# A fourth inner pair in seven products in every second gate and up group, and matrix products of the MLP tied to written order

## Chip, core and metric

The kernel runs on one core of one Trainium2 chip. The time is device time in microseconds (us), the median of several executions of the one program; before the change it is 1436.71 us (three runs, 1436.64 to 1439.13). Five engines work side by side, each through its own queue of instructions: TensorE (PE in the profile, its weight loads PEld), VectorE (DVE), ScalarE (ACT), GpSimd (POOL) and SyncE (SP, which here only issues transfers). Semaphores make one engine wait for another.

## The reference

One layer of an encoder over 256 rows of width 2048 in float32: four mixers side by side, cross attention, and the SwiGLU MLP that this change touches.

```python
D_MODEL = 2048
SEQ = 256
D_FF = ((8 * D_MODEL // 3 + 255) // 256) * 256      # 5632
...
def swiglu(h, w_gate_up, w_down):
    gate, up = jnp.split(h @ w_gate_up, 2, axis=-1)
    return (jax.nn.silu(gate) * up) @ w_down

def reference(x, mem, norm_g, w_in, ...):
    ...
        x = x + mix @ w_out[l]
        x = x + cross_attention(rms_norm(x, norm_g[l, 1]), mem_n, w_xq[l], w_xkv[l], w_xo[l])
        x = x + swiglu(rms_norm(x, norm_g[l, 2]), w_gate_up[l], w_down[l])
    return rms_norm(x, final_norm_g)
```

## The kernel before

**A product in three matmuls.** Float32 precision comes from splitting. Each operand is a high part (rounded to the type fp32r by a cast) and a low part (what the cast left). A product is high by high, high by low and low by high: the three matmuls of `part`, lines 433 to 435, each 128x128 by 128x512. Line 434 is the one that reads the low part `wl` of the weights.

**The weights as a stream.** The host lays all weights out in the order in which they are used, in slabs of 128x2048 (16 blocks of 128 columns). `Stream._load` fetches a slab into `raw` (three buffers); `Stream._half` casts 1024 columns of it to `wh` on ACT (line 135) and forms `wl` = `raw` − `wh` on DVE (line 136). Such a piece of `wh` and `wl` is called a half here. Four halves have buffers at a time: three of `wp` and one of `extra`. So the cast of a half can start only when TensorE is through with the half four places before it.

**Plain and paired slabs.** A group of the gate and up product takes 512 columns of gate and 512 of up, over 16 inner blocks of 128 (k), for 2 halves of the rows. A slab holds four blocks (k, column). Its plan has one letter per slab. "N", plain: 4 blocks by 2 row halves is 8 products, 24 matmuls, in two halves of the weights. "S", paired: two k by two column halves by two row halves by Winograd's variant of Strassen's scheme, 7 products in place of 8, 21 matmuls. Sums of weight blocks take the place of four of the blocks and sums of activations (`combine`, into the tiles `z`) the place of the activations. A paired slab makes four halves, or phases, 0 to 3: 1024, 512, 1024 and 1024 columns, used by 6, 3, 6 and 6 matmuls (`Stream._sums`, cast in line 159, low part in line 160). Before phase 2, DVE adds up weights in place in `raw` (line 157): four additions of 128x512, each reading what an earlier one wrote. Where the slab is in `SUMMED`, two transfers (`two`, line 101) and one accumulating transfer that POOL issues (line 102) do half of it, and DVE has two additions left.

**The groups.** Group 0 of gate and up is all plain (`gemm_rows`); while it runs, `combined` makes the sums of activations in the background. Groups 1 to 10 run the plan `GROUP` = "NNSNSNSN": five plain slabs and three paired ones, all three in `SUMMED`. After its last paired slab and at its end a group has a row of work on DVE: `mixed` puts the products together (four operations of 128x512), `gated` adds to the gate, `upped` adds to the up part, `up` multiplies (line 287) and `store_turned` transposes (line 557): twelve operations of 128x512. The result goes to memory in transposed order and is fetched back and split by the background task `fetch` (f and act tiles, 128x256) as operands of the down product.

**Down.** Two passes over 1024 columns each (`PASSES`), with the four-addition form of "S". The activation sums are made as they are needed; the last of the seven right operands (`x4` in `paired_rows`) is written into the slot of the first of the two inner blocks. `down_end` ends the kernel: four matmuls with the identity (line 1244) add what `mixed` left in `split` to the second half of the rows, then twelve inner blocks run for the first half of the rows, then for the second, each followed by `norm`.

**What sets the order.** The framework (Tile) places the instructions in each engine's queue when the program is built, by its own estimate of when each is ready; on the chip each queue runs in that order. `keep_place` adds edges without semaphores that tie an instruction behind the one written before it on the same engine. Before the change `down_end` has them around its four identity matmuls, and nothing ties the products of `paired_rows`.

Of the kernel before, what the change touches and what calls it, by code (L numbers as in the profile page):

```python
# [14 lines left out]
F32R = mybir.dt.float32r  # L15
# [8 lines left out]
P = 128  # L24
# [3 lines left out]
DFF = 5632  # L28
# [13 lines left out]
LATE = 12  # L42

GATE_UP = 1920 // 16 + 8
GROUP = "NNSNSNSN"

DOWN = GATE_UP + 80
PASSES = "NNNNSNNSNNSNNSNNSNNSNN", "NSNSNSNSNSNSNSNSNSNNNN"

PAIRED = {a + i for a, plan in [(GATE_UP + 8 * j, GROUP) for j in range(10)] + [(DOWN, PASSES[0]), (DOWN + 22, PASSES[1])]  # L50
          for i, x in enumerate(plan) if x == "S"}
SUMMED = {i for i in PAIRED if i < DOWN}

LAG, OWED, SOON, FAR = 1.3, 0.9, 0.01, 18.0
V_NG = 0
# [16 lines left out]
class Stream:  # L72
# [39 lines left out]
    def _half(self):  # L112

        nc, n = self.nc, self.made
        if n % 16 == 0 and self.phase == 0:
            self._load(n)
        if n // 16 in PAIRED:
            return self._sums()
# [74 lines left out]
    def take_sums(self, w, ks, cols):  # L193

        assert self.n // 16 in PAIRED and self.n % 16 == 0
        self.order += [(w, ks[k], cols[c] + i * P) for k, c in ((1, 0), (0, 0), (1, 1), (0, 1)) for i in range(4)]
# [58 lines left out]
class Block:  # L255
# [208 lines left out]
    def paired_rows(self, w, cols, slots, sums, plan, mixed, first, ready=None, late=0, before=None, swap=False):  # L464

        st, s, nk = self.st, len(sums), len(slots)  # L470
        rest = [k for k in range(nk) if not any(k in ks for ks, _ in sums)]
        steps = [(c, k) for c in range(2) for k in rest]
        todo, q = iter(sums), {}
        count = {"a0": len(rest) + s, "a1": len(rest) + s, "b0": len(rest) + s, "b1": len(rest)}
        left, total = {}, 0

        def put(name, hi, lo, wh, wl):
            if name not in q:
                for x in [name] if name in count else "1675":
                    q[x] = (self.bank if (name in count) == swap else self.gbank)()  # L480
                    left[x] = count.get(x, s)
            new = left[name] == count.get(name, s)
            left[name] -= 1
            self.part(q[name][:, :], hi, lo, wh, wl, new, left[name] == 0)

        form = lambda t, r: (t[:, r * P:(r + 1) * P], t[:, R + r * P:R + (r + 1) * P])
        n = done = 0
        for i, kind in enumerate(plan):
            if before:
                before(i)  # L490
            if kind == "S":
                ks, z = next(todo)
                a = [form(slots[ks[0]], 0), form(slots[ks[1]], 0), form(slots[ks[1]], 1)]
                hi, lo, x4 = self.forms(z, slots[ks[0]])
                x1, s2, s3 = ((hi[:, i * P:i * P + P], lo[:, i * P:i * P + P]) for i in range(3))
                t = (("5", x1), ("7", s3))
                pairs = iter((("1", a[0]), ("b0", x4), ("a0", a[1]), *(t if st.n // 16 in SUMMED else t[::-1]), ("a1", a[2]), ("6", s2)))
                for parts in st.take_sums(w, ks, cols):
                    for wh, wl in parts:
                        name, (hi, lo) = next(pairs)  # L500
                        put(name, hi, lo, wh, wl)
                        self.bg.poll()
                done += 1
                if done == s:
                    mixed(*(q[i] for i in "1567"))
            else:
                for c, k in steps[n:n + 4]:
                    if ready:
                        ready(k)
                    wh, wl = st.take(w, k, cols[c], 4)  # L510
                    for r in range(2):
                        put("ab"[c] + str(r), *form(slots[k], r), wh, wl)
                        self.bg.poll()
                n += 4
            if first and done == s and n >= len(rest):
                first(q["a0"], q["a1"])
                first = None
        assert n == len(steps) - late and done == s
        return [q["b0"], q["b1"]], rest[len(rest) - late:]
# [527 lines left out]
    def gate_up(self, gp, f, z):  # L1047

        nc = self.nc
        box, g, stored = {}, {}, []  # L1050

        def gate(ps):
            for r in range(2):
                g[r] = gp.tile([P, 512], F32, name=f"g{r}", tag=f"g{r}")
                nc.scalar.activation(g[r], ps[r], AF.Silu, scale=box["col"][:, r:r + 1])

        def up(j, ps, h=None):
            h = h or [gp.tile([P, 512], F32, name="h", tag="h", bufs=2) for _ in range(2)]
            for r in range(2):
                self.stt(h[r], ps[r], box["col"][:, r:r + 1], g[r], ALU.mult, ALU.mult)  # L1060
                self.store_turned(self.ff, 4 * j, r, g[r], h[r])
            stored.append(self.bg.now)

        def mixed(q1, q5, q6, q7):

            g[0], g[1], h[0], h[1] = (gp.tile([P, 512], F32, name=n, tag=n, bufs=b) for n, b in (("g0", 1), ("g1", 1), ("h", 2), ("h", 2)))
            nc.scalar.copy(g[0], q1)
            self.tt(h[0], g[0], q6, ALU.add)
            self.tt(g[1], h[0], q7, ALU.add)
            self.tt(h[0], q5, h[0], ALU.subtract)  # L1070
            self.tt(h[1], q5, g[1], ALU.subtract)

        def gated(*ps):

            for r in range(2):
                self.tt(g[r], g[r], ps[r], ALU.add)
                nc.scalar.activation(g[r], g[r], AF.Silu, scale=box["col"][:, r:r + 1])

        def upped(j, ps):

            for r in range(2):
                self.tt(h[r], h[r], ps[r], ALU.add)
            up(j, h, h)

        h = {}

        def fetch(k0, k1, ahead, pause, wait=0):

            m = {}
            for k in range(k0, k1 + ahead):  # L1090
                if k < k1:
                    while len(stored) <= k // 4:
                        yield
                    m[k] = self.tmp()
                    self.load_turned(m[k], self.ff, k)
                if k >= k0 + ahead:
                    while wait and self.bg.now < stored[(k - ahead) // 4] + wait:
                        yield
                    mark = self.mark()
                    self.split(f[k - ahead], m.pop(k - ahead))  # L1100
                    self.keep_place(mark)
                    self.have = k - ahead + 1
                    yield pause

        def norm():

            mark = self.mark()
            nc.scalar.activation(self.mg[:, 0:1], self.mg[:, 0:1], AF.Silu)
            self.keep_place(mark)
            yield 2.0  # L1110
            self.row_norm(1, box)
            yield

        arrival = lambda: gp.tile([P, R], F32, name="ar", tag="ar", bufs=4)
        last = self.bg.add(self.arrive(self.xf[1], 3, arrival, self.put3, FAR), go=True)
        col = self.bg.add(norm())

        def combined():
            for ks, z in sums:
                yield 3.0  # L1120
                yield from self.combine(z, *(self.h3[k] for k in ks))

        sums = [((2 * i, 2 * i + 1), z[i]) for i in range(GROUP.count("S"))]
        comb = self.bg.add(combined())
        ps = self.gemm_rows("w_gate_up", [0, DFF], self.h3,
                            parts=[(range(8), [0]), (range(8, 12), [0]), (range(12), [1]), (range(12, 16), [0]), (range(12, 16), [1])],
                            before=lambda n: n in (1, 3) and self.bg.drain(self.late if n == 1 else last))
        self.bg.drain(col)
        gate(ps[0])
        up(0, ps[1])  # L1130
        early = self.bg.add(fetch(0, FT - 22, 3, 2.0, 15))
        self.bg.drain(comb)
        for j in range(1, DFF // 512):
            upped(j, self.paired_rows("w_gate_up", [j * 512, DFF + j * 512], self.h3, sums, GROUP, mixed, gated, swap=j % 2 == 0)[0])
        self.bg.drain(early)
        self.fetch = self.bg.add(fetch(FT - 22, FT, 6, SOON))

# [73 lines left out]
    def down_end(self, f, ss, ps, rest, split):  # L1211
# [29 lines left out]
        mark = self.mark()  # L1241
# [7 lines left out]
        for r in range(2):  # L1249
# [4 lines left out]
            for c in range(3):  # L1254
                x = self.half(c, r)
                self.stt(x, x, 0.375, fg[:, c * 512:(c + 1) * 512], ALU.mult, ALU.mult)
        nc.scalar.mul(fg[:, 3 * 512:4 * 512], fg[:, 3 * 512:4 * 512], 0.375)
        for r in range(2):
            for k, wh, wl in held:
                self.part_rows(ps[r], r, f[k], wh, wl, False, k == FT - 1)  # L1260
            norm(ps[r], r)


# [627 lines left out]
```

## Time and profile before

| | |
|---|---|
| median of 3 runs | 1436.71 us |
| the profiled execution's own time | 1435.07 us |
| its span in the trace | 1433.3 us |
| TensorE, busy share of the span, instructions | 99%, 6589 |
| VectorE | 80%, 1738 |
| ScalarE | 57%, 1183 |
| GpSimd | 16%, 306 |
| granted TensorE clock | 0.999 |
| groups 1 to 10 of gate and up | about 778 to 1193 us of the span |
| down | about 1193 to 1424 us |

In the profile, a row of the timeline gives the start in us, the duration in us, engine, line, operation, output<-inputs (buffer numbers left out), shapes and count, and in brackets the idle time before it with what ended it. Durations overlap where an engine is pipelined: a matmul of 128x512 has a duration of 0.39 us, and the next starts 0.227 us after it. The time that an operation costs is therefore read from start to start. A row of the windows view gives the busy time of PE, PEld, DVE, ACT and POOL in that stretch with the count of instructions, then the granted clock, the busy share of the DMA engines and GB/s.

### The profile page before, as it was taken

How to read it: one execution, taken by the hardware profiler on the slowest of the kernel's cores; microseconds unless marked ns; L12 is line 12 of the kernel's file. 1: busy time of each engine (PE TensorE's matmuls, PEld its weight loads, DVE VectorE, ACT ScalarE, POOL GpSimd, SP SyncE). 2: the span in 40 equal slices, each digit the busy share in tenths (PEclk: the TensorE clock that was granted, in tenths of full speed). 3: DMA queues.
4: the chain of work that ended last, by engine and by line, in shares of the span. 5: the costliest groups of instructions: out<-in, count | busy, mean ns of one | idle time of the engine just before them, and what ended most of it. 6: DMA issues, size and time to landing. Idle time of an engine off the chain costs nothing.

```text
span 1433.3 us, 18652 instructions
## 1 busy us (share of the span) xinstructions
PE 1423.0 (99%) x6589; PEld 1180.7 (82%) x6589; DVE 1146.2 (80%) x1738; ACT 815.2 (57%) x1183; POOL 234.8 (16%) x306
## 2 busy tenths in 40 slices
PE   9999999999999999999999999999999999999997
PEld 8888888888888888888888888888888888888886
DVE  6667868777877767777677888898888888989997
ACT  7556565446645555556554656555555556655655
POOL 0000100013212223531431121122011002000000
PEclk9999999999999999999999999999999999999999
DMA  9876564546667788964986999889999887655554
GB/s 352 299 285 248 205 206 162 175 169 224 202 196 236 234 267 252 274 200 166 289 239 209 286 286 277 278 275 282 294 293 288 268 260 229 219 230 179 193 218 147
DMA packets 73037, 343.79 MB, mean 240 GB/s; under 512 B 10957, under 2 KB 12654, under 8 KB 45168
## 3 DMA queue, kind: packets, MB, share of 16 engines
q1 hardware_dynamic: 54848, 288.98, 57.5%
q0 software_dynamic: 17664, 52.97, 15.8%
q8 instruction: 51, 0.84, 0.2%
q10 hardware_dynamic: 432, 0.66, 0.1%
q14 instruction: 42, 0.34, 0.1%
HBM read 322.12 MB, written 20.45 MB: 239 GB/s over the span
## 4 chain that ended last, share of the span: by engine, by line
PE 97%; DVE 1%; ACT 0%; DMA 0%; issue 0%; SPq 0%; ACTq 0%
PE pg L433 22%; PE pg L434 22%; PE pg L435 22%; PE pm L434 7%; PE pm L435 7%; PE pm L433 7%; PE pg L381 4%; PE pg L382 2%; PE pm L1344 1%; PE pm L1022 1%; PE pm L993 1%; DMA raw<-in_W 0%; PE pm L1753 0%; DVE res L283 0%; PE pm L994 0%
## 5 line engine op out<-in xcount | busy, mean ns | idle before, releaser
L136 DVE TENSOR_TENSOR wl<-raw,wh 128x1024 fp32r<-128x1024 f32 (+1 forms) x413 | 494.8, 1212 | 166.1 <-ACT wh L135 163.2
L135 ACT CAST wh<-raw 128x1024 fp32r<-128x1024 f32 (+1 forms) x413 | 424.5, 1043 | 283.9 <-PE pg L435 196.4
L433 PE MATMUL pg<-wh,act 128*128 128x512 f32 (+1 forms) x1191 | 465.6, 391 | 0.0
L434 PE MATMUL pg<-wl,act 128*128 128x512 f32 (+1 forms) x1191 | 463.9, 389 | 0.4 <-DVE wl L136 0.2
L435 PE MATMUL pg<-wh,act 128*128 128x512 f32 (+1 forms) x1191 | 463.9, 389 | 0.0
L433 PEld LDWEIGHTS pg<-wh,act 128*128 128x128 f32 x1191 | 223.8, 188 | 47.8 <-issue 1.5
L434 PEld LDWEIGHTS pg<-wl,act 128*128 128x128 f32 x1191 | 223.8, 188 | 47.2 <-DVE wl L136 1.3
L435 PEld LDWEIGHTS pg<-wh,act 128*128 128x128 f32 x1191 | 223.7, 188 | 47.2 <-DVE act L283 0.4
L159 ACT CAST wh<-raw 128x1024 fp32r<-128x1024 f32 (+1 forms) x150 | 137.0, 921 | 146.8 <-DVE raw L157 46.4
L160 DVE TENSOR_TENSOR wl<-raw,wh 128x1024 fp32r<-128x1024 f32 (+1 forms) x150 | 156.1, 1061 | 57.0 <-ACT wh L159 56.8
L434 PE MATMUL pm<-wl,act 128*128 128x512 f32 x309 | 120.5, 390 | 0.1
L433 PE MATMUL pm<-wh,act 128*128 128x512 f32 x309 | 120.2, 389 | 0.0
L435 PE MATMUL pm<-wh,act 128*128 128x512 f32 x309 | 120.2, 389 | 0.0
L381 PE MATMUL pg<-act,wh 128*128 128x512 f32 x256 | 90.5, 395 | 0.0
L382 PE MATMUL pg<-act,wl 128*128 128x256 f32 x256 | 71.8, 280 | 0.0
L434 PEld LDWEIGHTS pm<-wl,act 128*128 128x128 f32 x309 | 58.0, 188 | 13.0 <-DVE wl L136 0.6
L433 PEld LDWEIGHTS pm<-wh,act 128*128 128x128 f32 x309 | 58.0, 188 | 12.0
L435 PEld LDWEIGHTS pm<-wh,act 128*128 128x128 f32 x309 | 58.0, 188 | 12.0
L102 POOL DMA_DIRECT2D two<-in_W x30 | 26.6, 887 | 241.2 <-DMA two<-in_W 116.0
L157 DVE TENSOR_TENSOR raw<-raw 128x512 f32<-128x512 f32 x90 | 62.0, 689 | 1.3
L159 ACT CAST wh<-two 128x1024 fp32r<-128x1024 f32 x30 | 31.6, 1052 | 51.1 <-PE pg L435 21.7
L381 PEld LDWEIGHTS pg<-act,wh 128*128 128x128 f32 x256 | 48.1, 188 | 10.5
(375 smaller groups left out, 1821.9 us busy)
## 6 DMA issues: line engine op xcount, KB each, us to landing
raw<-in_W SPq DMA_DIRECT2D x216, 1024.0 KB, 5.6
raw<-in_W SPq DMA_DIRECT2D x30, 768.0 KB, 6.1
two<-in_W SPq DMA_DIRECT2D x60, 256.0 KB, 4.9
two<-in_W POOLq DMA_DIRECT2D x30, 512.0 KB, 9.3
raw<-in_W SPq DMA_DIRECT2D x11, 512.0 KB, 7.6
hidden<-g POOLq DMA_DIRECT2D x22, 256.0 KB, 3.7
tmp<-hidden POOLq DMA_DIRECT2D x44, 128.0 KB, 5.4
features<-tmp POOLq DMA_DIRECT2D x32, 128.0 KB, 5.3
```

Source lines behind the costliest of these rows:

```text
L102: nc.gpsimd.dma_start(t, W[:, 512:1536], accum_op=ALU.add)
L135: nc.scalar.copy(wh[:, a:b], r[:, a:b])
L136: nc.vector.tensor_tensor(out=wl[:, a:b], in0=r[:, a:b], in1=wh[:, a:b].bitcast(F32), op=ALU.subtract)
L157: nc.vector.tensor_tensor(out=out, in0=a, in1=b, op=ALU.add)
L159: nc.scalar.copy(wh, src)
L160: nc.vector.tensor_tensor(out=wl, in0=src, in1=wh.bitcast(F32), op=ALU.subtract)
L381: self.nc.tensor.matmul(p[:, :], wh, slot[:, :], start=start, stop=False)
L382: self.nc.tensor.matmul(p[:, 0:R], wl, slot[:, 0:R], start=False, stop=stop)
L433: self.nc.tensor.matmul(p, hi, wh, start=start, stop=False)
L434: self.nc.tensor.matmul(p, hi, wl, start=False, stop=False)
L435: self.nc.tensor.matmul(p, lo, wh, start=False, stop=stop)
L993: nc.tensor.matmul(p[:, :], q[d][:, r * P:(r + 1) * P], kt[d][:, :], start=d == 0, stop=False)
```

## The change

Every second group gets a plan with four paired slabs: "NSNSsNSN", in groups 2, 4, 6, 8 and 10. The small "s" is a paired slab that isn't in `SUMMED`: its weights come in one plain transfer and DVE makes all four additions. A fourth tile `z3` takes the activation sums of the fourth pair, made in group 0. Each product in `paired_rows`, and the products of `down_end`, are tied to written order by `keep_place`.

```diff
-GROUP = "NNSNSNSN"
+GROUPS = "NNSNSNSN", "NSNSsNSN"
...
-PAIRED = {a + i for a, plan in [(GATE_UP + 8 * j, GROUP) for j in range(10)] + [(DOWN, PASSES[0]), (DOWN + 22, PASSES[1])]
-          for i, x in enumerate(plan) if x == "S"}
-SUMMED = {i for i in PAIRED if i < DOWN}
+PAIRED = {a + i for a, plan in [(GATE_UP + 8 * j, GROUPS[j % len(GROUPS)]) for j in range(10)] + [(DOWN, PASSES[0]), (DOWN + 22, PASSES[1])]
+          for i, x in enumerate(plan) if x in "Ss"}
+SUMMED = {GATE_UP + 8 * j + i for j in range(10) for i, x in enumerate(GROUPS[j % len(GROUPS)]) if x == "S"}
...
+            mark = self.mark()
             self.part(q[name][:, :], hi, lo, wh, wl, new, left[name] == 0)
+            self.keep_place(mark)
...
-            if kind == "S":
+            if kind in "Ss":
...
-        sums = [((2 * i, 2 * i + 1), z[i]) for i in range(GROUP.count("S"))]
+        z = z + [gp.tile([P, 1024], F32R, name="z3")]
+        sums = [((2 * i, 2 * i + 1), z[i]) for i in range(4)]
...
-            upped(j, self.paired_rows("w_gate_up", [j * 512, DFF + j * 512], self.h3, sums, GROUP, mixed, gated, swap=j % 2 == 0)[0])
+            plan = GROUPS[(j - 1) % len(GROUPS)]
+            upped(j, self.paired_rows("w_gate_up", [j * 512, DFF + j * 512], self.h3, sums[:8 - plan.count("N")], plan, mixed, gated,
+                                      swap=j % 2 == 0)[0])
...
         for r in range(2):
+            mark = self.mark()
             for k, wh, wl in held:
                 self.part_rows(ps[r], r, f[k], wh, wl, False, k == FT - 1)
+            self.keep_place(mark)
             norm(ps[r], r)
```

## The prediction

> **What bounds the kernel now.** I read the page's busy times, then its chain, then the windows over the MLP.
>
> ```profile
> span 1433.3 us, 18652 instructions
> PE 1423.0 (99%) x6589; PEld 1180.7 (82%) x6589; DVE 1146.2 (80%) x1738; ACT 815.2 (57%) x1183; POOL 234.8 (16%) x306
> PE 97%; DVE 1%; ACT 0%; DMA 0%; issue 0%; SPq 0%; ACTq 0%
> ```
>
> TensorE is busy from end to end and holds 97% of the chain. A matmul that goes saves its time, and a matmul that waits adds its wait; nothing else counts. What matters is how far VectorE, which must have `wl` ready, is from becoming late.
>
> ```profile
> 750.00:775.00 25.00, 25.00 (x112) 20.68 (x112) 17.93 (x27) 14.40 (x20) 0.00 (x0) 1.00 0.58 200
> ...
> 975.00:1000.00 25.00, 25.00 (x112) 20.71 (x111) 22.84 (x29) 14.83 (x18) 5.86 (x7) 1.00 0.86 260
> ```
>
> In the all-plain group 0 DVE works 17.9 of 25 us; in the mixed groups 22.8. The mean leaves 2 us, but four halves of buffer are all the slack there is, so the order inside a group decides. That it is short of slack already shows in the chain, in group 4:
>
> ```profile
> 914.50 1.06 ACT wh L159
> 915.58 1.24 DVE wl L160
> 916.86 0.50 PE pm L434
> ```
>
> That is phase 3 of the first paired slab: PE waited there for the low part, and the slab had two plain slabs before it.
>
> **Removed matmuls.** Each fourth pair turns 24 matmuls into 21. Five groups: 15 fewer. Window 975 to 1000 holds 112 matmuls in 25 us, 0.223 each; the rows below (985.58 to 993.51, 35 steps) give 0.2266. So **−3.4 us**. The transferred bytes are the same, and the new activation sums run in group 0, under the idle 7 us in 25 of its DVE: nothing.
>
> **First paired slab of a changed group.** Group 6 begins at 985.58 in the trace and is one of the changed. I lay the built program's new DVE queue on its old times.
>
> ```profile
> 985.58 0.39 PE L433 MATMUL pm<-wh,act 128*128 128x512 f32 x1
> ...
> 993.51 0.39 PE L435 MATMUL pm<-wh,act 128*128 128x512 f32 x1
> ```
>
> ```profile
> 993.98 1.05 ACT L159 CAST wh<-two 128x1024 fp32r<-128x1024 f32 x1 [1.78 <-issue]
> ```
>
> ```profile
> 978.14 3.50 DVE L136 TENSOR_TENSOR wl<-raw,wh 128x1024 fp32r<-128x1024 f32 x3 [0.21 <-ACT wh L135]
> ...
> 985.72 1.23 DVE L136 TENSOR_TENSOR wl<-raw,wh 128x1024 fp32r<-128x1024 f32 x1
> 986.87 0.68 DVE L283 TENSOR_TENSOR g<-g,pg 128x512 f32<-128x512 f32 x1
> ...
> 991.20 1.19 DVE L136 TENSOR_TENSOR wl<-raw,wh 128x1024 fp32r<-128x1024 f32 x1
> 992.31 1.82 DVE L160 TENSOR_TENSOR wl<-raw,wh 128x1024 fp32r<-128x1024 f32 x2
> 994.04 0.42 DVE L283 TENSOR_TENSOR f<-tmp,f 128x256 fp32r<-128x256 f32 x1
> 994.38 0.69 DVE L157 TENSOR_TENSOR raw<-two,raw 128x512 f32<-128x512 f32 x1
> 995.07 1.23 DVE L160 TENSOR_TENSOR wl<-two,wh 128x1024 fp32r<-128x1024 f32 x1
> 996.21 0.69 DVE L157 TENSOR_TENSOR raw<-raw 128x512 f32<-128x512 f32 x1
> ...
> 998.09 1.23 DVE L160 TENSOR_TENSOR wl<-raw,wh 128x1024 fp32r<-128x1024 f32 x1 [1.19 <-ACT wh L159]
> ```
>
> Reading them: a matmul started at 993.51 was the last on its half, and the cast into that buffer came at 993.98, so a buffer is free 0.24 us after the half's time (993.74) is over. DVE runs without a pause from 978.14 to 996.9: that is the previous group's tail, of which 4.33 us (986.87 to 991.20) stand in one piece. From start to start a half costs DVE 1.14 us (and is done 0.1 later), a short one 0.60, an addition 0.69, or 0.61 where nothing hangs on it. Phase 3 is ready at 999.3, and PE reads it at 985.58 + 48 + 15 + 1 matmuls = 1000.1: 0.8 us to spare.
>
> In the new plan one plain slab is gone from in front: PE wants phase 3 at 985.58 + 40 × 0.2266 = 994.65. The same tail ends at 991.20 (the slot at 985.72 now holds the slab's phase 0). Then phase 1 (0.60), addition (0.61), phase 2 (1.14), addition (0.69): 994.24. The cast (1.05) ends at 995.4, and the built queue puts both halves of the *next* plain slab in front of phase 3 in groups 2, 6 and 10 (slab and phase after each `wl`, "add" for line 157):
>
> ```
> ... transposes; wl 1S.1; add; wl 1S.2; add; wl 2N.a; wl 2N.b; wl 1S.3; wl 3S.0 ...
> ... wl 4s.0; wl 4s.1; add; add; add; add; wl 4s.2; wl 5N.b; wl 4s.3; wl 5N.a ...
> ```
>
> 994.24 + 3 × 1.14 + 0.1 = 997.75: **3.1 us** late. In groups 4 and 8 one half is in front: 995.5 + 1.14 + 0.1, 2.1 us late. (With none it would be 2.0: the tail alone does that.)
>
> **The "s" right behind an "S".** Its phase 0 takes the buffer of the S's phase 0 and all four additions wait for it.
>
> ```profile
> 1393.28 2.87 DVE L157 TENSOR_TENSOR raw<-raw 128x512 f32<-128x512 f32 x4
> 1396.06 1.22 DVE L160 TENSOR_TENSOR wl<-raw,wh 128x1024 fp32r<-128x1024 f32 x1
> ```
>
> Four additions cost 2.78. From the end of S's phase 0: release 0.24, cast 1.05, low part 1.14, short one 0.60, additions 2.78, phase 2 1.14, 0.1: 7.05 us. PE needs it after 3 + 6 + 6 + 6 + 3 + 1 matmuls, 5.67: **1.4 us** late. Then one half of the next slab and phase 3, 2.28 us, against six matmuls, 1.36: **0.9** more. Between the two places N gives DVE time to catch up, so they add: 5.4 us in three groups, 4.4 in two, **+25.0 us**. Bounds: if only one of the two places waits, 11 to 14; nothing hidden and weights late, up to 5 more, since a 1 MB transfer took
>
> ```profile
> raw<-in_W SPq DMA_DIRECT2D x4, 1024.0 KB, 7.5
> ```
>
> 7.5 us to land, and the "s" slab's is issued only when phase 3 of the first S is done, some 8 us before its cast. I take nothing for it.
>
> **Moved splits.** `fetch` now splits in the plain groups' last third; one 128x256 split (0.34 by the row at 994.04) falls into the tail before four of the five: **+1.3** (0 to 2).
>
> **Edges.** In gate and up the queue was in written order already; 0. In down the old queue ran other products while the operand `x4` was late:
>
> ```profile
> 1231.16 0.39 PE L433 MATMUL pg<-wh,act 128*128 128x512 f32 x1
> ...
> 1234.03 0.40 PE L435 MATMUL pg<-wh,act 128*128 128x512 f32 x1
> ```
>
> ```profile
> 1232.08 1.22 DVE L160 TENSOR_TENSOR wl<-raw,wh 128x1024 fp32r<-128x1024 f32 x1
> ...
> 1233.55 0.29 DVE L283 TENSOR_TENSOR act<-tmp,act 128x128 fp32r<-128x128 f32 x1
> ```
>
> Its last matmul stands at 1234.03, and by written order it is due at 1231.62. The new DVE queue does two operations of 0.34 before `x4` and one of 1.14 after it, so it comes at 1233.4: 1.8 late, less 0.3 lost there already, **+1.5** (0 to 2). DVE then has that time at the next pair, where 0.3 was lost: −0.3.
>
> At the end the old queue put 13 products of the first and second half of the rows before or between the identity matmuls, which wait for DVE:
>
> ```profile
> 1406.98 0.39 PE L433 MATMUL pm<-wh,act 128*128 128x512 f32 x1
> ...
> 1410.55 0.77 PE L1244 MATMUL pm<-tmp,identr 128*128 128x256 f32 x2
> 1411.15 0.39 PE L433 MATMUL pm<-wh,act 128*128 128x512 f32 x1
> ...
> 1424.30 0.39 PE L435 MATMUL pm<-held,act 128*128 128x512 f32 x1
> ```
>
> ```profile
> 1410.45 0.43 DVE L283 TENSOR_TENSOR tmp<-res,tmp 128x256 fp32r<-128x256 f32 x1
> ```
>
> The last identity matmul needs 1410.45 + 0.43. Tied, all 72 products start behind it: 1411.05 + 71 × 0.2266 = 1427.14 in place of 1424.30, **+2.8** (0 to 3.4; two DVE operations before it also change places).
>
> **Sum**: −3.4 + 25.0 + 1.3 + 1.2 + 2.8 = +26.9 on the profiled execution's 1435.07 (1.8 of it outside its span): 1462. The median of the runs shown is 1.6 above that execution: **1463.6**.
>
> **Rivals.**
> Faster: if DVE ran its queue far enough ahead at both places in a group, only −3.4 and the edges (+4.0 by the rows, 0 if the old reordering there bought nothing) would be left: 1433 to 1437. For it: DVE idles 2.2 us in 25, 3.6 in a group, plain groups could make up the rest, and an "s" slab needs only 4.5 more (3 × 1.14 + 0.60 + 2.78, against 2 × 1.14). Against: the slack is not where the work is; phase 3 had 0.8 us to spare and loses 5.4. It decides if phase 3 is ready by 994.65.
> Half: one place waits, the other is absorbed: 1436.7 − 3.4 + 13 + 5 = 1451.
> Weights late as well, 1 us at each of five "s" and as much behind them: 1463.6 + 10 = 1474. The 7.5 us above against 8 speak for it, that the landings in the groups before held up no matmul against it.
> Half clock: after a wait of 3 us the array could run slow. At the program's start it did:
>
> ```profile
> 5.72 0.40 PE L434 MATMUL pg<-wl,act 128*128 128x256 f32 x1
> 5.93 0.31 PE L435 MATMUL pg<-wh,act 128*128 128x256 f32 x1
> 6.08 0.28 PE L433 MATMUL pg<-wh,act 128*128 128x256 f32 x1
> 6.20 0.28 PE L434 MATMUL pg<-wl,act 128*128 128x256 f32 x1
> ```
>
> 0.21 a step, then 0.12, about 5 us into the work. Up to 5 us at half speed after each of five long waits costs 2.5 each: 1476. Against it: the waits are broken by matmuls. [...]
>
> **Chances.** Forecast, both places (1456 to 1471): 0.55. Half: 0.20. Late weights or half clock: 0.16. Faster rival: 0.09, of which 0.06 ends faster by over 0.2% (2.9 us, about what a measurement of this kernel tells from none) and 0.03 within it. Slower 0.91. The range, 1447 to 1475, leaves out the faster rival, the low end of Half and the top of the last: 0.19.
>
> **What would show it.** PE waiting for line 160 in phase 3 of the first S and in phases 2 and 3 of "s", five times each, about 5 us a group; plain groups still 41.5 us; the last matmul some 3 us later behind line 1244. It is wrong if changed groups last 40.8 us, or if waits stand mostly at DMA.

## The result, and the profile after

The changed kernel takes 1472.83 us (median of five runs, 1471.7 to 1475.43) against 1436.64 (five runs, 1435.42 to 1439.13): a ratio of 1.0252, 95% interval 1.0237 to 1.0267. It is 36.2 us slower, where 26.9 were forecast. The profiled execution took 1475.43 us.

From the page of the kernel after: the span, the busy times, the chain by engine, and the group of the low-part matmuls of the paired slabs.

```profile
span 1473.7 us, 18659 instructions
PE 1436.6 (97%) x6574; PEld 1181.1 (80%) x6574; DVE 1170.0 (79%) x1776; ACT 825.5 (56%) x1195; POOL 234.7 (16%) x306
PE 85%; DVE 8%; DMA 4%; issue 1%; ACT 1%; SPq 0%; ACTq 0%; DVEq 0%
L434 PE MATMUL pm<-wl,act 128*128 128x512 f32 x279 | 112.3, 402 | 11.7 <-DVE wl L160 11.7
```

There are 15 matmuls fewer and TensorE is busy 13.6 us longer, its share falls from 99% to 97%. VectorE's part of the chain goes from 1% to 8%, DMA's from 0% to 4%. The last row names the place: TensorE stood 11.7 us in front of matmuls that read `wl`, each time for line 160.

Windows of the kernel after, one row for each of groups 2, 3, 4, 6, 8 and 10:

```profile
820.13:866.69 46.56, 42.70 (x182) 33.47 (x180) 39.43 (x47) 23.08 (x27) 7.75 (x9) 1.00 0.87 256
866.69:908.17 41.48, 41.48 (x185) 34.35 (x183) 36.74 (x46) 25.74 (x32) 7.74 (x9) 1.00 0.93 286
908.17:955.98 47.81, 44.39 (x181) 34.42 (x180) 40.05 (x48) 24.61 (x28) 7.78 (x9) 0.96 0.84 250
997.46:1044.35 46.89, 42.70 (x182) 33.48 (x180) 40.12 (x48) 24.27 (x28) 5.99 (x7) 1.00 0.85 245
1085.83:1135.75 49.92, 45.67 (x182) 35.23 (x181) 41.71 (x51) 25.92 (x29) 5.88 (x7) 0.93 0.82 235
1177.23:1227.73 50.50, 44.53 (x181) 34.53 (x180) 40.90 (x50) 26.48 (x30) 4.28 (x5) 0.97 0.68 213
```

The plain group 3 lasts 41.48 us, as before, for 183 matmuls: 0.2267 each. A changed group has 180, nominally 40.81. What each has over that is 5.75, 7.01, 6.08, 9.11 and 9.70 us: 37.65 in five groups, of which 3.4 are given back by the matmuls saved. In groups 4, 8 and 10 the granted clock is under 1, of which more below. The last matmul starts at 1465.28, 40.98 after that of before (1424.30). The account: 0.96 ahead of group 1 (which starts between 777.7 and 779.4 in the profiles of this case, with and without the new plan); 33.7 in the groups; 1.4 in the first pass of down (118.03 us against 116.65); 4.95 in the second pass and the end.

The first paired slab of group 6, TensorE's timeline and then VectorE's (start and duration in us):

```profile
1004.94 0.39 PE L433 MATMUL pg<-wh,z 128*128 128x512 f32 x1
1005.81 0.50 PE L434 MATMUL pg<-wl,z 128*128 128x512 f32 x1 [0.48 <-DVE wl L160]
...
1006.84 0.39 PE L435 MATMUL pg<-wh,z 128*128 128x512 f32 x1
1007.50 0.50 PE L433 MATMUL pm<-wh,act 128*128 128x512 f32 x1 [0.27 <-ACT wh L159]
1009.82 0.50 PE L434 MATMUL pm<-wl,act 128*128 128x512 f32 x1 [1.82 <-DVE wl L160]
```

```profile
1003.37 0.65 DVE L160 TENSOR_TENSOR wl<-raw,wh 128x512 fp32r<-128x512 f32 x1
1003.94 0.68 DVE L157 TENSOR_TENSOR raw<-two,raw 128x512 f32<-128x512 f32 x1
...
1005.68 0.68 DVE L157 TENSOR_TENSOR raw<-raw 128x512 f32<-128x512 f32 x1
1006.28 2.35 DVE L136 TENSOR_TENSOR wl<-raw,wh 128x1024 fp32r<-128x1024 f32 x2
1008.55 2.35 DVE L160 TENSOR_TENSOR wl<-raw,wh 128x1024 fp32r<-128x1024 f32 x2
```

This is the queue that the prediction laid out: the two low parts of the next plain slab (line 136, at 1006.28) stand ahead of phase 3's at 1008.55, and TensorE, which began phase 3 at 1007.50, goes on at 1009.82. Phase 2 and the start of phase 3 had waited before (0.64 and 0.43 us by start to start). These waits belong to the same lateness: the slab is 3.44 us over nominal in all, and the prediction had phase 3 come 3.1 us late. By the same count the first pair is 3.09, 2.37, 3.44, 5.35 and 5.84 us over nominal in groups 2, 4, 6, 8 and 10. In groups 8 and 10 its weights came late. ScalarE in group 8 (from 1085.83), ScalarE in group 10 (from 1177.23), and VectorE behind the second:

```profile
1087.13 1.05 ACT L159 CAST wh<-raw 128x1024 fp32r<-128x1024 f32 x1 [3.64 <-DMA raw<-in_W]
```

```profile
1178.63 1.05 ACT L159 CAST wh<-raw 128x1024 fp32r<-128x1024 f32 x1 [4.62 <-DMA raw<-in_W]
```

```profile
1179.71 1.22 DVE L160 TENSOR_TENSOR wl<-raw,wh 128x1024 fp32r<-128x1024 f32 x1 [1.27 <-ACT wh L159]
```

The cast of the pair's phase 0 waits for the transfer, VectorE waits for the cast, and the rest of the previous group's row stands behind that low part in VectorE's queue. Phase 1's low part, which follows the row, came 5.6 to 5.9 us after the group's start in groups 2, 4 and 6 (5.91 in the rows above) and 7.9 and 8.0 us after it in groups 8 and 10. Behind an "S", the "s" of the same group:

```profile
1023.62 0.50 PE L433 MATMUL pg<-wh,z 128*128 128x512 f32 x1
1025.05 0.50 PE L434 MATMUL pg<-wl,z 128*128 128x512 f32 x1 [0.93 <-DVE wl L160]
...
1026.32 0.40 PE L433 MATMUL pm<-wh,act 128*128 128x512 f32 x1
1027.32 0.50 PE L434 MATMUL pm<-wl,act 128*128 128x512 f32 x1 [0.61 <-DVE wl L160]
```

0.25 before the first row, 1.20 and 0.78 after the two rows of line 433 (step less 0.2267): phase 2 and phase 3, about 2.5 us with the small rest in four of the five groups, against 2.3 forecast. Group 4 has 4.48: its wait before the first row's place is 1.14 in place of 0.25, and half clock (0.50, from 936.46) follows.

The end, TensorE's timeline:

```profile
1443.46 0.39 PE L435 MATMUL pm<-wh,act 128*128 128x512 f32 x1
1444.46 0.38 PE L1249 MATMUL pm<-tmp,identr 128*128 128x256 f32 x1 [0.61 <-ACT tmp L299]
1445.97 0.38 PE L1249 MATMUL pm<-tmp,identr 128*128 128x256 f32 x1 [1.13 <-DVE tmp L283]
1446.85 0.85 PE L1249 MATMUL pm<-tmp,identr 128*128 128x256 f32 x2 [0.49 <-ACT tmp L299]
...
1448.46 0.62 PE L434 MATMUL pm<-wl,act 128*128 128x512 f32 x1
1448.88 0.63 PE L435 MATMUL pm<-wh,act 128*128 128x512 f32 x1
```

The four identity matmuls (now line 1249) come one by one, each as its operand is ready: 0.78 + 1.40 + 0.76 + 0.35 = 3.3 us. Then eight matmuls run at 0.426 us a step, 1.6 us more.

### The profile page after: what moved, and what is told of

Read it like the earlier page. It is cut to its first block, busy times and chain, and to the rows that moved or that the text cites. A ratio compares the mean times of both kernels' runs of the same rounds, so it can differ in the third digit from the quotient of the medians.

```text
span 1473.7 us, 18659 instructions
## 1 busy us (share of the span) xinstructions
PE 1436.6 (97%) x6574; PEld 1181.1 (80%) x6574; DVE 1170.0 (79%) x1776; ACT 825.5 (56%) x1195; POOL 234.7 (16%) x306
## 4 chain that ended last, share of the span: by engine, by line
PE 85%; DVE 8%; DMA 4%; issue 1%; ACT 1%; SPq 0%; ACTq 0%; DVEq 0%
PE pg L433 20%; PE pg L435 20%; PE pg L434 20%; PE pm L434 5%; PE pm L435 5%; PE pm L433 5%; DMA raw<-in_W 4%; PE pg L381 4%; DVE wl L160 3%; PE pg L382 2%; DVE wl L136 2%; DVE raw L157 2%; PE pm L1351 1%; ACT wh L159 1%; PE pm L1024 1%
## 5 line engine op out<-in xcount | busy, mean ns | idle before, releaser
L136 DVE TENSOR_TENSOR wl<-raw,wh 128x1024 fp32r<-128x1024 f32 (+1 forms) x403 | 483.0, 1211 | 163.6 <-ACT wh L135 161.5
L135 ACT CAST wh<-raw 128x1024 fp32r<-128x1024 f32 (+1 forms) x403 | 414.9, 1042 | 280.2 <-PE pg L435 190.3
L159 ACT CAST wh<-raw 128x1024 fp32r<-128x1024 f32 (+1 forms) x170 | 156.0, 923 | 172.3 <-PE pg L435 66.1
L160 DVE TENSOR_TENSOR wl<-raw,wh 128x1024 fp32r<-128x1024 f32 (+1 forms) x170 | 177.7, 1061 | 53.9 <-ACT wh L159 53.7
L434 PE MATMUL pm<-wl,act 128*128 128x512 f32 x279 | 112.3, 402 | 11.7 <-DVE wl L160 11.7
L433 PE MATMUL pm<-wh,act 128*128 128x512 f32 x279 | 111.2, 399 | 1.4 <-ACT wh L159 1.4
L435 PE MATMUL pm<-wh,act 128*128 128x512 f32 x279 | 110.7, 397 | 0.0
L157 DVE TENSOR_TENSOR raw<-raw 128x512 f32<-128x512 f32 x110 | 75.6, 687 | 1.8
L434 PEld LDWEIGHTS pm<-wl,act 128*128 128x128 f32 x279 | 53.4, 191 | 27.5 <-DVE wl L160 16.5
L102 POOL DMA_DIRECT2D two<-in_W x30 | 26.9, 896 | 255.9 <-DMA two<-in_W 76.0
L433 PEld LDWEIGHTS pm<-wh,act 128*128 128x128 f32 x279 | 53.7, 193 | 15.1 <-ACT wh L159 3.6
L435 PEld LDWEIGHTS pm<-wh,act 128*128 128x128 f32 x279 | 53.7, 192 | 10.9
```

What stands on the lines that cost most here:

```text
L102: nc.gpsimd.dma_start(t, W[:, 512:1536], accum_op=ALU.add)
L135: nc.scalar.copy(wh[:, a:b], r[:, a:b])
L136: nc.vector.tensor_tensor(out=wl[:, a:b], in0=r[:, a:b], in1=wh[:, a:b].bitcast(F32), op=ALU.subtract)
L157: nc.vector.tensor_tensor(out=out, in0=a, in1=b, op=ALU.add)
L159: nc.scalar.copy(wh, src)
L160: nc.vector.tensor_tensor(out=wl, in0=src, in1=wh.bitcast(F32), op=ALU.subtract)
```

## Experiments

Theory at the start: the waits at the two places carry the loss, and the edges cost only in down and at the end. Rivals: the edges cause most of it; the fetch, moved by the new plan, makes weights late. All medians stand beside runs of the kernel before on the same chip (1436.2 to 1436.8).

| kernel | median, us | over before | ratio, 95% |
|---|---|---|---|
| both places of edges, old plan | 1444.96 | 8.6 | 1.0044 to 1.0080 |
| edges of the rows, old plan | 1438.51 | 2.1 | 1.0009 to 1.0027 |
| edges, identity matmuls later | 1439.86 | 3.5 | 1.0018 to 1.0037 |
| new plan, no edges | 1455.56 | 19.2 | 1.0120 to 1.0152 |
| only an early first pair, no edges | 1445.14 | 8.8 | 1.0033 to 1.0070 |
| only an "s" behind an "S", no edges | 1442.64 | 6.3 | 1.0028 to 1.0054 |
| new plan, no edges, stream order | 1457.15 | 20.8 | 1.0118 to 1.0155 |
| new plan, no edges, fetch spread | 1456.14 | 19.8 | 1.0103 to 1.0151 |
| new plan, edges of the rows | 1467.87 | 31.1 | 1.0201 to 1.0232 |
| after, fetch spread | 1466.67 | 29.9 | 1.0191 to 1.0228 |
| after, stream order | 1465.18 | 29.0 | 1.0175 to 1.0227 |
| four summed pairs, two plain slabs in front, no edges | 1463.25 | 26.5 | 1.0169 to 1.0203 |

**Edges alone.** The plan of before with the edges of after.

```diff
+            mark = self.mark()
             self.part(q[name][:, :], hi, lo, wh, wl, new, left[name] == 0)
+            self.keep_place(mark)
...
+            mark = self.mark()
             for k, wh, wl in held:
                 self.part_rows(ps[r], r, f[k], wh, wl, False, k == FT - 1)
+            self.keep_place(mark)
```

> The kernel before with both places of edges and without the new plan: no matmul is saved or moved inside the groups. Theory: the edges cost by themselves. The down passes lose the 1.2 us of the prediction (the profile of after showed 118.03 against 116.65 us for pass 0), the end 2.8 us by the queue of products behind the identity matmuls, and up to 5 us if the wait is again followed by eight matmuls at 0.426 us a step, as at 1448.46 us in the profile of after. Sum +4 to +6.5 us, 1441 to 1443. The groups stay at 41.48 us each. Rival: the end of after came late for reasons that lie in the groups (cast and evict work handed on), and the edges alone cost nothing: 1436 to 1437.

With the first of the two places alone:

> The kernel before with the edges of paired_rows alone, the end unbound. Theory: the down passes lose 1.2 us (the operand x4 of a paired slab is waited for with nothing let past it), the groups nothing since their order is the written one already: 1437.5 to 1438.5. Rival: the edges of the rows are free, 1436 to 1437, and then all that the edges cost is at the end. The difference from the run with all edges is the end's: 2.8 us by the prediction, 4.4 to 5 with the half clock.

Measured +8.6 and +2.1. The edges in down cost somewhat more than the theory's 1.2 (the first pass alone is 1.45 longer, 118.10 us against 116.65); the end is 6.4 us by the difference, above the theory's 2.8 and above the 4.4 to 5. The profile with both shows 4.58 of it in the second pass (119.15 against 114.57), with one stretch of eight matmuls at half clock (steps of 0.42 us from 1417.34 on); it is 1444.52 in a spread of 1442.5 to 1448.4, so what the end costs differs from run to run. Over their nominal time all ten groups together are 2.8 and 0.9 us in the two profiles (0.6 in that of before), 2.1 of the 2.8 in one group: with the old plan the edges cost next to nothing in the groups.

**The end's cause.** The identity matmuls moved between the first and the second half of the rows, within the bound order.

```diff
-        mark = self.mark()
-        for j, parts in split:
-            for a in parts:
-                nc.tensor.matmul(ps[1][:, j:j + R], self.identr, a, start=False, stop=False)
-        self.keep_place(mark)
...
             mark = self.mark()
+            for j, parts in split if r else ():
+                for a in parts:
+                    nc.tensor.matmul(ps[1][:, j:j + R], self.identr, a, start=False, stop=False)
             for k, wh, wl in held:
```

> The kernel before with both places of edges, but the identity matmuls stand between the first and the second half of the rows, inside the bound order. Theory: the end lost its time because the identity matmuls were ahead of all 72 products and their operand, made by GpSimd, VectorE and ScalarE, is late there; behind 36 products (8.2 us at 0.2267) it is there in time. So the end is as before, no half clock near the end, and the time is 3 to 5 us under the run with all edges: 1437 to 1439. Rival: the held products' own order is what costs, and the time is that of the run with all edges.

Its timeline at the identity matmuls (here line 1259):

```profile
1419.81 0.40 PE L435 MATMUL pm<-held,act 128*128 128x512 f32 x1
1420.05 0.63 PE L1259 MATMUL pm<-tmp,identr 128*128 128x256 f32 x4
1420.52 0.40 PE L433 MATMUL pm<-wh,act 128*128 128x512 f32 x1
```

All four in one go, with no wait and no half clock (the next steps are 0.23 to 0.24 us): 5.1 us less than with the edges alone. The place of the identity matmuls in the bound order is the cause. It ends 0.9 above the theory's 1437 to 1439: the second pass still takes 1.0 us more than before, in waits of 0.95 and 0.20 for VectorE's `held` and `wl`.

**The plan alone.** After, without any of the new edges.

```diff
-            mark = self.mark()
             self.part(q[name][:, :], hi, lo, wh, wl, new, left[name] == 0)
-            self.keep_place(mark)
...
-            mark = self.mark()
             for k, wh, wl in held:
...
-            self.keep_place(mark)
```

> The kernel after without any of the new edges: the plan alone. Theory: the waits of the five changed groups carry the loss. From the profile of after these are 37.6 us over the nominal time of their matmuls, less 3.4 us for 15 matmuls saved, so +30 to +34 us, 1466 to 1470; the end of the last pass as before. Rival 1: without edges TensorE takes other ready products into the waits (the planner may put an identity or a later product ahead), and the groups lose under 15 us: 1445 to 1452. Rival 2: the edges cause most of the loss, 1437 to 1440.

Measured +19.2: none of the three. It is below the theory's 30 to 34 and above the first rival's range, though that rival's mechanism is what the trace shows. The five changed groups are 4.99, 4.87, 4.95, 2.94 and 3.12 us over nominal, 20.9 in place of 37.65. TensorE's timeline at the same place of group 6 shows where the rest went:

```profile
1004.07 0.50 PE L433 MATMUL pm<-wh,act 128*128 128x512 f32 x1 [0.47 <-ACT wh L159]
1004.40 0.39 PE L433 MATMUL pg<-wh,z 128*128 128x512 f32 x1
1004.63 0.40 PE L434 MATMUL pm<-wl,act 128*128 128x512 f32 x1
...
1007.15 0.39 PE L434 MATMUL pg<-wl,z 128*128 128x512 f32 x1
```

Phase 3 begins as in after (line 433 at 1004.07 and 1004.40), but its low-part matmul of `z` is only at 1007.15. Between the two run products of the next plain slab, whose low parts VectorE has made first:

```profile
1002.84 2.36 DVE L136 TENSOR_TENSOR wl<-raw,wh 128x1024 fp32r<-128x1024 f32 x2
1005.11 2.36 DVE L160 TENSOR_TENSOR wl<-raw,wh 128x1024 fp32r<-128x1024 f32 x2
```

VectorE's order at this place is the same with and without the edges. It suits a TensorE that goes past the late product; the edges take that away and leave VectorE's order as it was. The first pass of down takes 118.28 us here, 1.6 more than before, without any new edge: in waits for `y` and `wl`, at other places than with the edges.

**Do plan and edges add up?** After, without the edges at the end.

```diff
-            mark = self.mark()
             for k, wh, wl in held:
...
-            self.keep_place(mark)
```

> The kernel after without the edges at its end: the new plan, and the products of paired_rows tied. Theory: plan and edges multiply. With the plan alone the five changed groups were 20.9 us over the nominal time of their matmuls, with plan and edges 37.6, because without edges TensorE's queue takes products of the next plain slab into the waits. So this run keeps most of the 37.6, and loses only the end's cost, 6.5 us by the difference of the two runs without the plan: 1465 to 1468. Rival: the groups' extra came from somewhere else (chance of one profile, half clock), plan and edges add up: 1455.6 + 2.1 = 1457 to 1458.

1467.87, in the theory's range. 31.1 less 19.2 for the plan and 2.1 for the rows' edges leaves **9.8 us that exist only together**; the rival had none. ScalarE's, VectorE's, GpSimd's and SyncE's queues are those of after, and TensorE's up to the end. The groups are 6.83, 5.79, 7.71, 5.11 and 7.17 over nominal, 32.6 in all: so the 1.3 to 4 us by which groups 4, 8 and 10 stood out in the profile of after belong to that execution and not to the program. By the profiles the 9.8 arises in the groups: 32.6 with rows' edges and plan, against 20.9 with the plan and 0.9 with the edges. The first pass of down takes 118.20 us, so what plan and edges each add to it alone (1.6 and 1.45) doesn't add up there.

**VectorE's order with TensorE free and tied.** Casts on ScalarE and low parts on VectorE tied to the order of the stream, first without TensorE's edges, then with all of them.

```diff
+        mark = len(nc.cur_bb.bb.instructions)
         nc.scalar.copy(wh, src)
         nc.vector.tensor_tensor(out=wl, in0=src, in1=wh.bitcast(F32), op=ALU.subtract)
+        self.chain(mark)
...
+    def chain(self, mark):
+        if not GATE_UP * 16 <= self.made < DOWN * 16 + 16:
+            return
+        for i in self.nc.cur_bb.bb.instructions[mark:]:
+            last = self.last.get(i.engine)
+            if last is not None:
+                self.tc.add_manual_dep(i, last.name, mybir.DependencyInfo(
+                    mybir.DependencyClass.NoSync, mybir.DependencyReason.DATA), reason="order")
+            self.last[i.engine] = i
```

> The plan alone without TensorE's edges; instead the casts on ScalarE and the low parts on VectorE are held in the order of the stream through the gate and up groups. Theory: halves of the next plain slab stand ahead of the first pair's last parts in VectorE's queue, which is the 1.1 us over the tail's 2.0 in groups 2, 6 and 10; with the order written the first pair loses 2.0 us and s 1.4, so the time falls by 5 to 15 us from the plan alone. Rival: the tail and the additions decide alone and the order is worth nothing, or holds casts back behind late weights: the same as the plan alone within 2 us, or slower.

> The kernel after with every edge, and beside them the casts on ScalarE and the low parts on VectorE held in the order of the stream through the gate and up groups, so that no half of a later slab stands ahead of an earlier slab's last part. TensorE's queue is that of after. Theory: with TensorE tied, each half put in front costs its 1.1 us. The wait for the first pair's phase 3 (2.1 us in groups 2, 6 and 10, 1.03 in 4 and 8) goes, and so does the one for the phase 3 of s (0.78 in all five): 12 us less than after, 1459 to 1464. With TensorE free the same order was worth nothing (1457.2 against 1455.6), since TensorE filled those waits with the very halves that stand in front. Rival: the order of VectorE is worth nothing here either, because the casts wait for TensorE anyway and the wait only moves to the next slab: 1471 to 1475.

| median, us | VectorE as built | VectorE in stream order |
|---|---|---|
| TensorE free | 1455.56 | 1457.15 |
| TensorE tied | 1472.83 | 1465.18 |

With TensorE free the order is worth nothing, as the rival had it; with TensorE tied it is worth 7.7 us, of the 12 expected, just outside the theory's range. In group 6 of the tied run, TensorE and then VectorE:

```profile
1007.17 0.51 PE L449 MATMUL pm<-wh,act 128*128 128x512 f32 x1 [0.34 <-ACT wh L163]
1008.43 0.51 PE L450 MATMUL pm<-wl,act 128*128 128x512 f32 x1 [0.76 <-DVE wl L164]
```

```profile
1005.28 0.68 DVE L160 TENSOR_TENSOR raw<-raw 128x512 f32<-128x512 f32 x1
1007.15 1.23 DVE L164 TENSOR_TENSOR wl<-raw,wh 128x1024 fp32r<-128x1024 f32 x1 [1.19 <-ACT wh L163]
1008.29 2.35 DVE L138 TENSOR_TENSOR wl<-raw,wh 128x1024 fp32r<-128x1024 f32 x2
```

The 2.09 us in front of phase 3's low part became 1.03, not 0: VectorE now idles 1.19 us for the cast, which needs the addition at 1005.28, and that addition is late behind the tail. In groups 4 and 8 the 1.03 stayed. The wait for the "s" slab's phase 3 (0.78) is gone in all five groups. Three times 1.06 and five times 0.78 are 7.1 us, about what the medians show; the groups are 26.3 us over nominal, against 32.6 in the run with the rows' edges, which has TensorE in the same order there.

**Each place by itself,** without edges and without a saved matmul: the first pair after one plain slab, then the "s" after two.

```diff
-GROUPS = "NNSNSNSN", "NSNSsNSN"
+GROUPS = "NNSNSNSN", "NSNSNNSN"
```

> The plan alone without edges, but the second plan is NSNSNNSN: three pairs as before, none of them the unsummed s, and one plain slab instead of two ahead of the first pair. No matmul is saved. Theory: the wait at the first pair is a term of its own, 2.1 to 3.1 us in each of five groups by the prediction and 3.1 to 5.8 in the profile of after: +11 to +20 us, 1448 to 1457, half clock where the wait passes 3 us. Rival: the wait at the first pair comes from s (its sums and parts queue on VectorE and push the group's work), and without s it is gone: 1436 to 1439.

```diff
-GROUPS = "NNSNSNSN", "NSNSsNSN"
+GROUPS = "NNSNSNSN", "NNSsNNSN"
```

> The plan alone without edges, but the second plan is NNSsNNSN: two plain slabs ahead of the first pair as before, and s right behind a pair. Three pairs, no matmul saved. Theory: s behind S costs 2.3 to 2.5 us in each of five groups, 11.5 to 12.5 us, and the first pair none: 1448 to 1449.5. Rival: s costs only because the first pair had put VectorE and ScalarE behind, and alone it costs under 1 us a group: 1437 to 1441.

+8.8 and +6.3. Both places cost by themselves, so both rivals fall; both cost less than the theory's 11 and more, again since TensorE is free here (1.1 to 2.3 us at the first pair, 1.2 to 1.9 at "s"). Together they make 15.1; the plan alone, with the 3.4 of saved matmuls put back, makes 22.6. Of the 7.5 between, the profiles show 4.2 at the two places: the first pair is 7.0 us over nominal in five groups by itself and 7.1 in the plan alone, the "s" 8.1 and 12.3. The rest is not assigned; the runs of each of these kernels spread by 3.7 to 4.5 us, and 1.5 more is in the first pass of down, which the plan alone lengthens (118.28 us) and the two others don't (116.75 and 116.30). The chain of the plan alone from 826 to 850 us, which is group 2, shows one way in which the first pair makes the "s" dearer:

```profile
by line: DMA raw<-in_W 34.0%; DVE raw L157 15.7%; DVE wl L160 13.0%; DVE wl L136 9.5%; issue 5.6%; PE pm L433 5.3%; PE pg L434 4.9%; ACT wh L159 4.4%; PE pg L435 4.3%; PE pg L433 1.8%; PE pm L434 1.8%; PE pm L435 1.2%; ACTq L159 0.2%
...
830.45 8.17 DMA raw<-in_W
```

The late first pair gives its `raw` buffer back late, the "s" slab's transfer is issued at 830.45 and lands 8.17 us later, and the four additions begin behind it: "s" costs 3.69 us there, 1.5 of it by half clock (steps of 0.43 us from 846.47 to 849.03 in the chain). This is the prediction's rival of late weights, in a run without the edges.

**The fetch.** Its pace eased from 0.9 to 9.0 in groups 1 to 10, first in the plan alone, then in after.

```diff
-            if self.owed < OWED and
+            if self.owed < self.limit and
...
         self.bg.drain(comb)
+        self.bg.limit = 9.0
         for j in range(1, DFF // 512):
```

> The plan alone without edges; the fetch of the first down weights is paced as a larger debt allows (limit 9.0 in place of 0.9), so that its loads and splits are spread over the groups instead of collecting in the plain ones' ends. Theory: the extra of groups 4, 8 and 10 over groups 2 and 6 (1.3, 3.0 and 3.6 us in the profile of after) comes from weights that land late because the fetch's loads share the queues with them there; with the loads moved, these groups fall to those of 2 and 6, and windows of half clock go: 6 to 10 us less than the plan alone. Rival: the weights land late because their buffers come free late behind the waits themselves, and the pace of the fetch changes under 2 us.

> The kernel after with every edge, but the fetch of the first down weights paced at a debt of 9.0 in place of 0.9, so that its loads no longer collect in the ends of the plain groups. Theory: in the profile of after the groups 4, 8 and 10 lost 1.3 to 4 us more than 2 and 6 because weights landed late beside the fetch's loads and TensorE, tied, could not go on; with the loads moved they fall to 5.5 to 6.5 us over nominal and the half clock behind them goes: 6 to 10 us less than after, 1463 to 1467. Rival: the weights are late since their buffers come free late, whatever the fetch does: within 2 us of after, 1471 to 1475.

0.6 us more than the plan alone, and 6.2 less than after. The amount with the edges is the theory's, the place is not: in the profile group 8 is still 8.73 over nominal and group 2 is 8.43; the sum over the groups is 33.7. That profile is the slowest of its four runs (1470.25), so it can't show where the median's 6.2 come from. In group 6 the new pace left one half in place of two in front of phase 3, and its wait fell from 2.09 to 1.03; that is the one part seen. That the fetch's loads make the weights late is not shown.

**Four pairs in better places?** Two plain slabs stay in front, and all four pairs have their sums half made by transfers.

```diff
-GROUPS = "NNSNSNSN", "NSNSsNSN"
+GROUPS = "NNSNSNSN", "NNSSNSSN"
```

> The plan alone without edges, the second plan NNSSNSSN: four pairs with 15 matmuls saved as in after, but two plain slabs stay ahead of the first pair, and the pair behind a pair has its sums half made by transfers like the others (two additions on VectorE in place of four). Theory: the places cost, not the number of pairs. From the end of the first pair's phase 0 the chain 0.24 + 1.05 + 1.14 + 0.60 + 1.39 + 1.14 + 0.1 is 5.66 us against TensorE's 5.67, so phase 2 is in time; phase 3 may be 0.9 us late, twice a group: changed groups 0 to 1.8 us over nominal, the time 1433 to 1442. Rival: four pairs are more than VectorE can carry in one group wherever they stand: 3 to 5 us over nominal each, 1448 to 1458.

1463.25, worse than the plan alone and beyond the rival too. Counted by slabs, the first pair loses 1.1 us in five groups, close to nothing as the theory had it. But of 21.2 us over nominal in the changed groups 19.1 stand at the second slab of the two pairs of "S" (5.2 at the first, 13.9 at the second), so an "S" behind an "S" stays dear with two additions in place of four. The changed groups are 2.7 to 6.3 us over nominal, about the rival's 3 to 5. Another 8.6 us are in the plain groups behind them (3.6 in group 7, 3.8 in group 9), which neither had. The chain from 1040 to 1056 us, the start of group 7:

```profile
by line: DMA raw<-in_W 58.6%; DVE wl L136 14.7%; PE pg L434 13.0%; PE pg L435 8.7%; PE pg L433 7.1%; ACT wh L135 6.6%; DVE g L557 4.6%; DVE h L287 4.5%; issue 3.7%; ACT wh L159 3.3%; DVEq L157 0.3%; ACTq L135 0.1%
...
1036.08 9.37 DMA raw<-in_W
```

A cast waited for weights that took 9.37 us to land. TensorE's wait for its low part is 0.46 us; the longer one in this group, 2.43 us, is for a low part that VectorE makes only after the row of the group before (lines 287 and 557 in the chain). A paired slab is used up in 21 matmuls, 4.76 us at 0.2267, but holds its `raw` buffer until its fourth phase; two in a row leave one buffer of three for the slabs behind. That explanation is argued from this chain and not shown; a kernel with a fourth `raw` buffer was not run. No version with four pairs came near the kernel before.

## Why the prediction came out as it did

The direction, the range and both places were right: five groups, phases 2 and 3, plain groups at 41.48. The size fell short by 9 us: 1472.83 lies above the main forecast (1456 to 1471) and inside the range only because that takes in part of the rivals with late weights and half clock. Both came, beside the forecast waits.

- **Removed matmuls**, −3.4: right; the groups' nominal time is 40.81 for 180.
- **First paired slab**, 13.5 forecast: 20.1 in the profile of after, 18.5 in the run with the rows' edges only. Where the weights came in time it was sized well: 3.09, 2.37 and 3.44 us in groups 2, 4 and 6 of after, against 3.1, 2.1 and 3.1. Missing was that the pair's own weights could land late and hold up the row on VectorE; the prediction considered late weights at the "s" alone and took nothing for them. By the time of phase 1's low part, against groups 2 and 6 of after, this is 2.0 to 2.4 us in each of groups 8 and 10 of after, and 0.8 to 1.1 in each of groups 2, 4 and 10 with the rows' edges only (in group 4 the trace doesn't tell what the cast waited for). Half clock adds 1.0 in group 8 of after, and 0.6 in group 6 of the other run.
- **"s" behind "S"**, 11.5 forecast: 12.5 with the rows' edges only, where no half clock fell on it. Right.
- **"Edges. In gate and up the queue was in written order already; 0."** This step failed. It holds for the old plan (the rows' edges alone cost 2.1 us, and leave the groups as they were within 0.3), but the working took the new plan's waits in written order without seeing that only the edges make TensorE wait like that. Without them it fills the waits with the next plain slab. Of the 36.2 us, 19.2 are the plan's, 9.8 exist only with both, 2.1 are down's and 5.0 the end's (1472.83 − 1467.87), each a difference of medians that spread by some 4 us. That the sum came near is luck as far as the plan goes: its waits were worked out for the tied order, which only the other half of the change brings about, and the ascription to the plan was wrong.
- **Edges in down**, +1.2: 2.1 by the run, with a wait for the late operand at the place that was named. In the combined kernel the first pass is 1.4 longer, but it's 1.6 longer with the plan alone, so that this 1.4 can't be put down to the edges.
- **The end**, +2.8: 5.0 to 6.4. The mechanism was right, as the moved identity matmuls show, and the size was off: the working took the last operand's time from before, but the four operands come in turn and hold TensorE 3.3 us, and half clock follows.
- **Moved splits**, +1.3: right in kind and too large. One split of 0.33 us stands ahead of the row in groups 4, 6, 8 and 10. In 4 and 6 VectorE doesn't idle behind it, and phase 1's low part comes 0.33 later than in group 2. In 8 and 10 it vanishes in VectorE's wait for the late weights. Why the spread fetch gives 6.2 back in the tied kernel and nothing in the free one is open.
- **Half clock** was a rival with a small share, argued down because "the waits are broken by matmuls". That it takes a wait of 3 us, as the prediction and one expectation had it, no run shows: in the profile of after no wait in the 3.41 us ahead of it was over 1.82 us. It came four times there, about 5.8 us in the groups by the steps over 0.2267 and 1.6 at the end, in place of the rival's 12.5; with the rows' edges only it came once before the end of the kernel (1.6). **Late weights** came too, ahead of the first pair as said, and at the "s" where the first pair was late.

## What to carry to other kernels

An order that a scheduler has built holds for the freedom it was built with: before tying one engine to written order, look at what the others' queues put in front at the places where it waits, or tie those too. A product saved is worth its matmuls only where the engine and the transfers that feed it have time at that place; a mean over the group, 2 us free in 25, does not say so. A wait worked out from queues holds where the weights are there in time; when a transfer lands late, every piece of work queued behind it moves with it, as behind the casts that waited 3.64 and 4.62 us in groups 8 and 10, and that needs a term of its own in the sum.

## What the runs showed of the hardware

In the profile of after the granted clock fell to 0.50 with no wait ahead of it as long as the stretch at 0.50 itself. Windows of that profile, PE's column first, the granted clock third from the end:

```profile
915.98:919.39 3.41, 1.98 (x7) 1.05 (x6) 3.41 (x5) 3.26 (x4) 1.16 (x2) 1.00 0.72 181
933.05:936.46 3.41, 1.50 (x6) 0.68 (x5) 3.34 (x5) 3.11 (x4) 0.47 (x1) 1.00 0.72 286
936.46:939.87 3.41, 3.41 (x9) 2.39 (x8) 3.41 (x4) 1.82 (x2) 0.41 (x1) 0.50 0.70 117
1189.05:1192.46 3.41, 1.33 (x6) 0.88 (x6) 3.41 (x4) 1.16 (x2) 0.00 (x0) 1.00 0.75 171
1192.46:1195.87 3.41, 3.41 (x10) 2.64 (x9) 2.34 (x4) 0.62 (x1) 0.91 (x1) 0.50 1.04 327
1264.14:1267.55 3.41, 1.83 (x9) 1.18 (x7) 3.41 (x10) 2.14 (x5) 0.00 (x0) 1.00 0.06 19
```

The stretches at half clock, as long as matmuls run, begin at 936.46, 1096.88, 1192.46 and 1448.46; they last 3.413 us, the second 6.83. Their distances, 160.42, 95.58 and 256.00 us, are 47, 28 and 75 times 3.413 us within 0.03, so in this trace they lie on one grid. In the 3.41 us ahead of each TensorE had no idle time over 1.82 us but only 6 matmuls by the view's count (7 at the end, four of them 256 wide) where 15 fit at 0.2267; windows with 7 and 9, at 915.98 and 1264.14, had full clock after them. The second of these holds most of the longest wait of the MLP, 2.12 us before 1268.10, so in this trace the longest single wait is not the one with half clock behind it. Counted by starts in windows of this grid, from 600 us on in the profile of after: the three with 4 or 5 matmuls of 512 columns had half clock after them; of the three with 6, those at 1093.47 and 1096.88 had it and that at 915.98 had not. A bound is not shown. A matmul at half clock takes 0.426 us in place of 0.2267 (the eight steps from 1448.46 on), so such a window costs about 1.6 us.
